# Zero fills on another engine, V's class-order transfers spread out, three products placed later: one encoder layer on one core

## The chip, the core and the metric

The kernel runs on one core of a Trainium2 chip. The core has a matrix engine (TensorE, PE), a vector engine (VectorE, DVE), an engine for activation functions (ScalarE, ACT), a general engine (GpSimd, POOL) and one that only issues transfers (SyncE, SP). Each engine executes its own instructions in order and waits at semaphores for the others. Transfers between the chip's memory and the core's are issued from an engine's queue (SPq, POOLq, ACTq) and carried out by 16 DMA engines. The metric is the device time of one execution, in microseconds (us).

## The reference

One layer of an encoder on x of shape 512 x 1024, float32. The parts that the change is near:

```
h = rms_norm(x, attn_norm_g)
xr, gate, q, k, v = split(h @ w_in)                  # 512 wide each
y_rnn  = (rg_lru(conv(xr), forward) + rg_lru(conv(xr), backward)) * gelu(gate)
y_attn = dilated_attention(q, k, v, rel_bias)        # 8 heads of 64
x = x + concat(rms_norm(y_rnn), rms_norm(y_attn)) @ w_out
x = x + square(relu(rms_norm(x) @ w_up)) @ w_down    # 4096 wide
return rms_norm(x) * final_norm_g
```

In `dilated_attention` a query looks at keys at three sets of distances: up to 64 in steps of 1, up to 256 in steps of 4, up to 1024 in steps of 16. The three softmaxes are put together by their denominators, which equals one softmax in which a key that lies in several sets counts several times.

## The kernel before

**Products.** A float32 operand is split into a high and a low part (`whi`, `wlo`: `conv_hi` on ScalarE, `conv_lo` on VectorE), and one product of a 128-row block is three matmuls (`mm3`, lines 312 to 314): high x high, high x low, low x high. Weights come in blocks of 128 x 1024 (512 KB).

**Stages.** First the projections of xr, V, gate, and Q and K of the first pair of heads, with the recurrent group's elementwise work beside them. Then attention, in pairs of heads p = 0 to 3. Then the attention half of the output projection, then the two halves of the feed-forward, whose products (`pu`, `pd`) run from about 230 us to the end.

**Attention.** Keys near a query (distance up to 64) and keys farther away (a multiple of 4) are scored apart: `att_s` computes the near scores (`pn`, line 779) for query blocks u, u+1 and, at u = 0, the far scores (`pf`, line 786). `att_f` adds the bias to the far scores of block u and writes them with their minimum into a tile `e` (line 799); `att_e` does so for the near scores (line 818), and ScalarE takes the exponential of the whole row in place (line 821). At the edges, blocks 0 and 3, 64 columns of `e` hold no score; they are filled with zero (line 803), since the transpositions that follow (`att_t`, line 833, results copied by ScalarE into `ett`, line 835) move whole 128 x 128 blocks. `att_av` multiplies with V: near blocks from `vs`, far ones from `vc`, V's rows in class order (position modulo 4), into which five transfers from `vs` sort them (`v_far`, line 723). Result `yp`, its square summed over pairs into `ysq`, its scaled copy `at`.

**Steps.** The loop goes over i = 0 to 4 and u = 0 to 3. Step (i, u) scores pair i (at u = 0 and 2) and transposes for pair i - 1; `att_av(i - 1)` stands at u = 3. In between, `fill` takes products off a queue of 80: 48 products of Q and K of pairs 1 to 3, then, after a call of `load_x`, 32 of the recurrent half of the output projection (`pwo<-whi,yh`). The table FILL says how many are taken at each of four places of a step, (1, 1, 1, 1) where it has no entry. Behind the loop come `att_av(3)`, more products, the column sums of `ysq` (`pcs`, line 411), from which the reciprocal roots `rcol` follow on VectorE, GpSimd and VectorE, and then the attention half (`pwo<-whi,oh`) in seven groups of four products, OSEQ: 11, s2, s3, s4, 21, s1, 22.

**Weight sums.** The groups s1 to s4 use sums of weight blocks. `load_x` loads a base block for each into `ws` from SP (line 1003) and adds others by accumulating transfers from GpSimd's queue (line 1005): s2 two, s3 one, s4 three, s1 one, in the order s2, s2, s3, s4, s4, s4, s1.

**What sets the order.** On TensorE, ScalarE, VectorE and GpSimd instructions run in the order in which the program is written. The queue of SP is put in order by the framework's scheduler from the data's dependences. GpSimd's queue holds, in program order, the zero fills, the accumulating transfers and the small power operation of the reciprocal roots (line 399).

## Time and profile before

| | |
|---|---|
| three runs | 553.13, 555.14, 554.56 us; median 554.56 us |
| profiled execution | 554.31 us, of it 552.5 us from the first to the last instruction (the span) |
| busy in the span | TensorE 530.6, VectorE 423.9, ScalarE 352.9, GpSimd 65.7 us |
| TensorE's waits over 1 us | 8.7 us for GpSimd, 2.2 and 1.3 us for VectorE, 1.1 us at the start |
| mean granted clock of TensorE | 0.981 |

Times in the profile are microseconds from the span's start. A row of the timeline gives start, duration, engine, line, operation, out<-in with partitions x elements, and a count; in brackets stands how long the engine sat idle before it and what ended that. Buffer numbers are left out of names. PEclk is the share of full speed that TensorE's clock was granted. Rows of matmuls that follow each other overlap: their starts say how fast they go.

### The profile page before, as it was taken

What the parts mean: (1) busy time and instruction counts of PE and PEld (TensorE: products, weight loads), DVE (VectorE), ACT (ScalarE), POOL (GpSimd) and SP (SyncE); (2) the same over time, 40 slices, a digit from 0 to 9 for tenths busy, and PEclk for the clock granted to TensorE, in tenths of its full rate; (3) what the DMA queues carried; (4) which work ended last, traced back from release to release, by engine and by line L of the source; (5) the groups of instructions that cost most, each with busy time, mean ns of one, the idle gap of its engine ahead of it and who ended that gap; (6) DMA issues with size and microseconds to landing.
All of it is one profiled execution on the core that took longest, in us unless ns stands there. A gap on an engine that the chain in (4) does not pass through costs nothing.

```text
span 552.5 us, 9169 instructions
## 1 busy us (share of the span) xinstructions
PE 530.6 (96%) x3507; PEld 452.7 (82%) x3507; DVE 423.9 (77%) x679; ACT 352.9 (64%) x557; POOL 65.7 (12%) x107
## 2 busy tenths in 40 slices
PE   9999999899999399999999999999999999999995
PEld 7856888687886367889999988888999999888884
DVE  6896886676764178789878988879857887986885
ACT  7668957657855253758657855557576776755664
POOL 3320000000010221000130031101011030131000
PEclk9999999999999689999999999999999999999998
DMA  7754169533299607774759599994897496799704
GB/s 268 233 156 130 35 174 198 141 98 101 85 332 302 127 12 157 239 286 152 191 134 218 172 222 274 277 339 162 261 268 195 149 187 177 180 306 256 191 0 152
DMA packets 34587, 104.10 MB, mean 188 GB/s; under 512 B 3981, under 2 KB 6954, under 8 KB 34544
## 3 DMA queue, kind: packets, MB, share of 16 engines
q1 hardware_dynamic: 26304, 74.66, 40.2%
q0 software_dynamic: 7920, 28.61, 27.6%
q8 instruction: 27, 0.44, 0.3%
q10 hardware_dynamic: 320, 0.25, 0.2%
q14 instruction: 16, 0.13, 0.1%
HBM read 96.15 MB, written 4.21 MB: 182 GB/s over the span
## 4 chain that ended last, share of the span: by engine, by line
PE 85%; DMA 7%; DVE 4%; ACT 1%; issue 1%; POOL 1%; SPq 0%; DVEq 0%; POOLq 0%; ACTq 0%
PE pu L314 10%; PE pu L312 10%; PE pu L313 10%; PE pd L314 9%; PE pd L312 9%; PE pd L313 9%; DMA ws<-in_w_out_dram 6%; PE pqk L312 3%; PE pqk L313 2%; PE pqk L314 2%; PE pg L502 2%; PE pv L312 1%; PE pt L833 1%; PE pv L314 1%; PE pv L313 1%; PE pp L314 1%
## 5 line engine op out<-in xcount | busy, mean ns | idle before, releaser
L268 DVE TENSOR_TENSOR wlo<-wraw,whi 128x1024 fp32r<-128x1024 f32 x73 | 89.0, 1221 | 29.9 <-ACT whi L260 29.6
L260 ACT ACTIVATE whi<-wraw 128x1024 fp32r<-128x1024 f32 x70 | 74.0, 1059 | 47.4 <-PE pd L314 20.5
L313 PE MATMUL pd<-wlo,ah 128*128 128x512 f32 (+1 forms) x195 | 75.2, 386 | 0.0
L312 PE MATMUL pd<-whi,ah 128*128 128x512 f32 (+1 forms) x195 | 75.2, 386 | 0.0
L314 PE MATMUL pd<-whi,al 128*128 128x512 f32 (+1 forms) x195 | 75.2, 386 | 0.0
L313 PE MATMUL pu<-hl,whi 128*128 128x256 f32 x224 | 63.4, 283 | 0.0
L314 PE MATMUL pu<-hh,wlo 128*128 128x256 f32 x224 | 63.4, 283 | 0.0
L312 PE MATMUL pu<-hh,whi 128*128 128x256 f32 x224 | 63.4, 283 | 0.0
L314 PE MATMUL pu<-h2h,wlo 128*128 128x256 f32 (+1 forms) x200 | 60.1, 301 | 0.2 <-DVE wlo L268 0.2
L312 PE MATMUL pu<-h2h,whi 128*128 128x256 f32 (+1 forms) x200 | 60.1, 300 | 0.0
L313 PE MATMUL pu<-h2l,whi 128*128 128x256 f32 (+1 forms) x200 | 60.0, 300 | 0.0
L260 ACT ACTIVATE whi<-tw 128x1024 fp32r<-128x1024 f32 x36 | 38.1, 1060 | 33.8 <-DMA tw<-in_w_up_dram 7.3
L268 DVE TENSOR_TENSOR wlo<-tw,whi 128x1024 fp32r<-128x1024 f32 x36 | 44.0, 1223 | 15.7 <-ACT whi L260 15.7
L312 PEld LDWEIGHTS pu<-hh,whi 128*128 128x128 f32 x224 | 43.0, 192 | 0.0
L313 PEld LDWEIGHTS pu<-hl,whi 128*128 128x128 f32 x224 | 43.0, 192 | 0.0
L314 PEld LDWEIGHTS pu<-hh,wlo 128*128 128x128 f32 x224 | 43.0, 192 | 0.0
L314 PEld LDWEIGHTS pd<-whi,al 128*128 128x128 f32 x195 | 36.6, 188 | 7.4
L313 PEld LDWEIGHTS pd<-wlo,ah 128*128 128x128 f32 x195 | 36.6, 188 | 7.4
L312 PEld LDWEIGHTS pd<-whi,ah 128*128 128x128 f32 x195 | 36.6, 188 | 7.3
L260 ACT ACTIVATE whi<-ts 128x1024 fp32r<-128x1024 f32 x24 | 25.5, 1061 | 24.7 <-PE pd L314 18.7
L314 PEld LDWEIGHTS pu<-h2h,wlo 128*128 128x128 f32 x200 | 38.3, 191 | 1.8 <-DVE wlo L268 0.6
L312 PEld LDWEIGHTS pu<-h2h,whi 128*128 128x128 f32 x200 | 38.3, 191 | 1.3
(265 smaller groups left out, 1234.6 us busy)
## 6 DMA issues: line engine op xcount, KB each, us to landing
wraw<-in_w_up_dram SPq DMA_DIRECT2D x25, 512.0 KB
ts<-in_w_dn_dram POOLq DMA_DIRECT2D x24, 512.0 KB, 13.7
wraw<-in_w_dn_dram SPq DMA_DIRECT2D x24, 512.0 KB
tw<-in_w_up_dram SPq DMA_DIRECT2D x15, 512.0 KB
tw<-in_w_up_dram POOLq DMA_DIRECT2D x15, 512.0 KB, 7.3
wraw<-in_w_in_dram SPq DMA_DIRECT2D x13, 512.0 KB
ts<-in_w_dn_dram SPq DMA_DIRECT2D x8, 512.0 KB
tw<-in_w_dn_dram SPq DMA_DIRECT2D x8, 512.0 KB
```

The lines of the kernel that those rows point to most:

```text
L260: act(hi, raws[i], AF.Copy)
L268: nc.vector.tensor_tensor(lo, r, f(splits[i][0]), op=OP.subtract)
L312: nc.tensor.matmul(o, lhsT=a[0], rhs=b[0], start=bool(first), stop=False, skip_group_check=on)
L313: nc.tensor.matmul(o, lhsT=a[0], rhs=b[1], start=False, stop=False, skip_group_check=on)
L314: nc.tensor.matmul(o, lhsT=a[1], rhs=b[0], start=False, stop=bool(last), skip_group_check=on)
L502: nc.tensor.matmul(pg[2 * d + j][halves[b ^ d]], lhsT=gwr[t][halves[b], c], rhs=xc[t][halves[b]], start=True, stop=True)
L833: nc.tensor.transpose(pt[:, i * P:(i + 1) * P], en[h][u][:, c * P:(c + 1) * P], ident)
```

## The change

Three things change, and the computation does not.

The zero fills of `att_f` (16 in all, 128 x 64) are issued on VectorE instead of GpSimd. `v_far` takes the block j as an argument and is called in steps (0, 0) to (0, 3) instead of for all j behind the gate projection. FILL takes three products instead of four in steps (3, 1), (3, 2) and (3, 3), moves the one product of step (4, 3) to its last place, and behind `att_av(3)` four are taken instead of three; what is left of the queue runs behind the column sums as before, three products instead of one.

```diff
@@ v_far
-    def v_far():
-        for j in range(4):
-            for a, b, s in (((0, P, 32 * j - 16),) if j else ((0, 64, 112), (64, P, 0))):
-                n = (b - a) // 4
-                nc.sync.dma_start(vc[s:s + n], vs[a:b, j, :])
+    def v_far(j):
+        for a, b, s in (((0, P, 32 * j - 16),) if j else ((0, 64, 112), (64, P, 0))):
+            n = (b - a) // 4
+            nc.sync.dma_start(vc[s:s + n], vs[a:b, j, :])
@@ behind the gate projection
-    v_far()
@@ att_f
-                nc.gpsimd.memset(t[:, g], 0.0)
+                nc.vector.memset(t[:, g], 0.0)
@@ the steps
-    FILL = {(4, 0): (0, 1, 0, 0), (4, 1): (0, 1, 0, 1), (4, 2): (0, 1, 0, 0), (4, 3): (0, 1, 0, 0)}
+    FILL = {(3, 1): (1, 1, 1, 0), (3, 2): (1, 1, 1, 0), (3, 3): (1, 1, 1, 0), (4, 0): (0, 1, 0, 0), (4, 1): (0, 1, 0, 1), (4, 2): (0, 1, 0, 0), (4, 3): (0, 0, 0, 1)}
     for i in range(5):
         for u in range(4):
+            if i == 0:
+                v_far(u)
@@ behind the steps
     att_av(3)
     att_y(3)
-    fill(3)
+    fill(4)
     cs = col_sums(ssy[1], "gs")
```

Lines behind `v_far` move up by one or two: the fill's line 803 becomes 801, the scores' 799 and 818 become 797 and 816.

GpSimd's queue around the weight sums `ws`, before: `e` is the score tile, `rcol` the reciprocal roots, first those of the recurrent half, then those of attention.

```order
L803 MEMSET e_1613 128x64
L803 MEMSET e_1617 128x64
L1005 DMA ws_1714<-in_w_out_dram 128x1024 x7
L803 MEMSET e_1850 128x64
L803 MEMSET e_1854 128x64
L803 MEMSET e_1909 128x64
L803 MEMSET e_1913 128x64
L399 TENSOR_TENSOR rcol_2_2206<-rv_2204,mhalf_85 128x4
L1097 DMA tw_2284<-in_w_up_dram 128x1024
```

And with the change:

```order
L399 TENSOR_TENSOR rcol_1_1579<-rv_1577,mhalf_85 128x4
L1003 DMA ws_1714<-in_w_out_dram 128x1024 x7
L399 TENSOR_TENSOR rcol_2_2199<-rv_2197,mhalf_85 128x4
L1097 DMA tw_2284<-in_w_up_dram 128x1024
L1097 DMA tw_2310<-in_w_up_dram 128x1024 x2
```

The sixteen fills are gone from it, among them four that stood behind the seven accumulating transfers.

VectorE in step (0, 1), before: from the recurrent group's last sum past the far scores of blocks 2 and 3 to the near scores of block 1, whose end frees the banks for the scores of blocks 2 and 3. `mf` and `mn` are the minima that go with the scores `e` (the numbers tell one buffer from another).

```order
L571 TENSOR_TENSOR gt_786<-gt_786,ga_470 128x512
L799 ISA e_1072,mf_1073<-pf_973,tw_641 128x128
L799 ISA mf_1073 128x1
L799 ISA e_1075,mf_1076<-pf_974,tw_644 128x128
L799 ISA mf_1076 128x1
L799 ISA e_1078,mf_1079<-pf_973,tw_641 128x128
L799 ISA mf_1079 128x1
L799 ISA e_1082,mf_1083<-pf_974,tw_644 128x128
L799 ISA mf_1083 128x1
L818 ISA e_1037,mn_1086<-pn_975,tw_641,mf_1038 128x256
L818 ISA mn_1086 128x1
```

And with the change:

```order
L571 TENSOR_TENSOR gt_786<-gt_786,ga_470 128x512
L797 ISA e_1070,mf_1071<-pf_970,tw_641 128x128
L797 ISA mf_1071 128x1
L797 ISA e_1073,mf_1074<-pf_971,tw_644 128x128
L797 ISA mf_1074 128x1
L797 ISA e_1076,mf_1077<-pf_970,tw_641 128x128
L797 ISA mf_1077 128x1
L801 MEMSET e_1076 128x64
L797 ISA e_1080,mf_1081<-pf_971,tw_644 128x128
L797 ISA mf_1081 128x1
L801 MEMSET e_1080 128x64
L816 ISA e_1034,mn_1084<-pn_972,tw_641,mf_1035 128x256
```

Two fills, those of block 3, stand here, and the two of block 0 stand in the same way in the group ahead of it; so it is in every pair.

SP's queue at the last of V's transfers (`vs<-vs`), before: `hs` are exchanges of the recurrent group, `wraw` weight blocks, `tw` the bias tables of the next pair.

```order
L243 DMA wraw_815<-in_w_in_dram 128x1024
L493 DMA hs_821<-ga_558 64x512 x2
L723 DMA vs_712<-vs_712 32x4x512
L243 DMA wraw_856<-in_w_in_dram 128x1024
L723 DMA vs_712<-vs_712 32x4x512
L243 DMA wraw_901<-in_w_in_dram 128x1024
L243 DMA wraw_938<-in_w_in_dram 128x1024
L243 DMA wraw_971<-in_w_out_dram 128x1024
L243 DMA wraw_1110<-in_w_out_dram 128x1024
```

And with the change:

```order
L243 DMA wraw_815<-in_w_in_dram 128x1024
L493 DMA hs_821<-ga_558 64x512 x2
L722 DMA vs_712<-vs_712 32x4x512
L243 DMA wraw_856<-in_w_in_dram 128x1024
L243 DMA wraw_896<-in_w_in_dram 128x1024
L243 DMA wraw_933<-in_w_in_dram 128x1024
L722 DMA vs_712<-vs_712 32x4x512
L243 DMA wraw_966<-in_w_out_dram 128x1024
L243 DMA wraw_1108<-in_w_out_dram 128x1024
```

The last of the five stands behind two more weight loads; the four ahead of it, of which the rows show one, keep their places.

## The prediction

> **What bounds the kernel now.** I read the page first, then the waits of TensorE, then its timeline at each wait, then the queue of the engine that ended the wait. From the page, the span and the busy times by engine:

> ```profile
> span 552.5 us, 9169 instructions
> PE 530.6 (96%) x3507; PEld 452.7 (82%) x3507; DVE 423.9 (77%) x679; ACT 352.9 (64%) x557; POOL 65.7 (12%) x107
> ```

> TensorE (PE) is busy for 96% of the span, so only its idle time, and the time in which it runs slowly, can be won. The longest of its waits (total us, times, longest):

> ```profile
> PE pt L833 <- POOL e L803: 8.7, 1, 8.7
> ```

> One transposition of exponentials (`att_t`) waits 8.7 us for a zero fill on GpSimd (POOL). Here it is in TensorE's timeline with the two next longest (start, duration, and in brackets the idle time before):

> ```profile
> 107.20 1.98 PE L779 MATMUL pn<-kraw,qraw 64*32 64x256 f32 x32 [2.21 <-DVE mn L818]
> ...
> 179.41 0.44 PE L833 MATMUL pt<-ident,e 128*128 128x128 f32 x2 [0.47 <-ACT ett L835]
> 188.51 1.54 PE L833 MATMUL pt<-ident,e 128*128 128x128 f32 x6 [8.66 <-POOL e L803]
> ...
> 202.71 1.23 PE L411 MATMUL pcs<-ones,ysq 128*128 128x1 f32 x8 [1.33 <-DVE ysq L588]
> ```

> ```profile
> 176.12:179.54 3.42, 2.35 (x16) 1.00 1.03 358
> 179.54:182.95 3.41, 0.30 (x2) 1.00 0.50 114
> ...
> 186.36:189.78 3.42, 1.27 (x7) 0.50 0.48 77
> 189.78:193.19 3.41, 3.41 (x12) 0.50 1.05 197
> ...
> 200.02:203.43 3.41, 2.08 (x13) 1.00 0.00 0
> 203.43:206.85 3.42, 3.42 (x10) 0.50 0.00 0
> ```

> The stretch from 200.02, with 1.33 us of idle, is followed by one at half speed; the stretch from 176.12, with 1.07 us, is not. A half-speed stretch that is busy throughout loses 1.7 us.

> **Part 1: the fills leave POOL.** This is what the 8.66 us stand behind, POOL's own timeline:

> ```profile
> 153.31 0.99 POOL L1005 DMA_DIRECT2D ws<-in_w_out_dram  x1 [10.23 <-DMA ws<-in_w_out_dram]
> ...
> 180.64 0.87 POOL L1005 DMA_DIRECT2D ws<-in_w_out_dram  x1 [13.62 <-DMA ws<-in_w_out_dram]
> 186.52 1.77 POOL L1005 DMA_DIRECT2D ws<-in_w_out_dram  x2 [5.00 <-DMA ws<-in_w_out_dram]
> 187.61 1.10 POOL L803 MEMSET e<- 128x64 f32 x4
> ```

> Seven weight sums are issued from POOL, and a sum waits for the landing of the one on which it builds. The last pair's four fills stand behind all seven and run at 187.61. On VectorE (DVE) each fill stands right behind the scores of its own tile, so nothing is left of this wait: **-8.7 us**. With it go the half-speed stretches behind it: 1.27 + 3.41 = 4.68 us busy at half speed are 2.34 us at full: **-2.3 us**. The 0.47 us ahead of 179.41, a wait for ScalarE, stays.

> What the fills cost on VectorE is not in the trace. The nearest rows, with minimum, median and maximum duration in ns:

> ```profile
> L143 DVE MEMSET ones<- x1: 165/165/165, 0.8 to 0.8; 128x128 f32 x1
> L145 DVE MEMSET epsb<- x1: 59/59/59, 1.0 to 1.0; 128x1 f32 x1
> L803 POOL MEMSET e<- x16: 141/152/849, 43.6 to 187.9; 128x64 f32 x16
> ```

> Between 59 and 165 ns a fill of 64 columns comes to 59 + 106 x 63/127 = 112 ns, an estimate. Four stand ahead of the second near-score group (`att_e`, u = 1) of every pair, and the scores of step 2 wait for that group. Where TensorE already waits, they lengthen the wait: the first pair, at 107.20, by 4 x 0.11 = **+0.4 us**. The bounds: 0.2 us if half of each fill hides under its neighbour, and 3.4 us at the 849 ns of POOL's slowest row. I take 0.4, since both VectorE rows lie far below POOL's slowest. The other pairs have cover. The rows below are, for pairs 1 to 3, the last score group on VectorE and the scores on TensorE that wait for it (0.99 us there, 1.98 us at 107.20, where the clock is half):

> ```profile
> 123.30 0.48 DVE L818 CUSTOM_DVE_ANT_0 e<-pn,tw,mf 128x256 f32<-128x256 f32 x1
> 125.46 0.99 PE L779 MATMUL pn<-kraw,qraw 64*32 64x256 f32 x32
> ...
> 142.92 0.48 DVE L818 CUSTOM_DVE_ANT_0 e<-pn,tw,mf 128x256 f32<-128x256 f32 x1
> 146.29 0.99 PE L779 MATMUL pn<-kraw,qraw 64*32 64x256 f32 x32
> ...
> 163.34 0.48 DVE L818 CUSTOM_DVE_ANT_0 e<-pn,tw,mf 128x256 f32<-128x256 f32 x1
> 166.16 0.99 PE L779 MATMUL pn<-kraw,qraw 64*32 64x256 f32 x32
> ```

> That leaves 1.7, 2.9 and 2.3 us; the last shrinks to 1.6, because part 3 takes one product away ahead of it. All exceed 0.4, so these twelve fills cost nothing.

> **Part 2: V's transfers.** The order of SP's queue shows that four of the five stay where they were; one goes behind two weight loads.

> ```profile
> 89.91 0.58 SPq L243 DMA_DIRECT2D wraw<-in_w_in_dram  x1
> 90.54 0.59 SPq L723 DMA_DIRECT2D vs<-vs  x1
> 91.23 4.74 SPq L243 DMA_DIRECT2D wraw<-in_w_in_dram  x2
> ...
> 98.72 1.06 ACT L260 ACTIVATE whi<-wraw 128x1024 fp32r<-128x1024 f32 x1 [3.85 <-DMA wraw<-in_w_in_dram]
> 99.81 1.22 DVE L268 TENSOR_TENSOR wlo<-wraw,whi 128x1024 fp32r<-128x1024 f32 x1 [3.19 <-ACT whi L260]
> 132.88 2.82 PE L914 MATMUL pav<-ett,vs 128*64 128x128 f32 x32
> ```

> The moved transfer, issued at 90.54, will be issued at about 96 (91.23 + 4.74); its reader starts at 132.88, 37 us later, so nothing is lost. Something could be won: the wait at 107.20 ends a chain on VectorE that follows the subtraction at 99.81, which waits for a load. But that is the load of 89.91, already ahead of the moved transfer. I take **0**. The bounds: no loss, and a gain of at most 1.6 us if the load should land so much earlier that the far scores start when theirs are done (99.3 instead of 100.9), which would leave 2.2 + 0.4 - 1.6 = 1.0 us of idle and so save the half-speed stretch too, 3.3 us in all.

> **Part 3: three products later.** TensorE's work is the same. Three products leave the last pair's steps 1 to 3; one of them now stands ahead of the column sums (`fill(4)` for `fill(3)`), two behind. A product is three matmuls 0.23 us apart, 0.69 us in all. Ahead of the sums runs this chain:

> ```profile
> 200.15 1.11 DVE L930 TENSOR_TENSOR yp<-pav,zrow 128x512 f32<-128x512 f32 x1
> 201.96 0.69 DVE L588 TENSOR_TENSOR ysq<-ysq 128x512 f32<-128x512 f32 x1 [0.70 <-ACT ysq L582]
> ...
> 200.53 0.39 PE L312 MATMUL pwo<-whi,yh 128*128 128x512 f32 x1
> 200.76 0.39 PE L313 MATMUL pwo<-wlo,yh 128*128 128x512 f32 x1
> ```

> The fourth product covers 0.69 of the 1.33 us; VectorE's order also has one weight subtraction (1.2 us) now behind `yp` instead of ahead of it. What is left lies between 0 and 0.64 us; I take 0.3: **-1.0 us**. That is below 1.07 us of idle, so the half-speed stretch from 203.43 goes as well: **-1.7 us**. Behind the sums three products instead of one stand over the reciprocal roots, where TensorE shows no wait even now. The moved products also carry the weight splits of groups 11, s2 and s3, and the split of 11 frees the buffer for this load:

> ```profile
> 172.34 0.33 SPq L243 DMA_DIRECT2D wraw<-in_w_up_dram  x1
> ```

> That split now stands behind `yp` on VectorE, so the load goes out some 5 us later, about 177; the feed-forward, which reads it, starts near 217 then, 40 us on.

> **What is late next.** With TensorE 13 us earlier the weight sums have less time. ScalarE reads the s4 sum at the first row below; the sum under it in the same tile took 5.35 us (from the chain of waits):

> ```profile
> 205.47 1.06 ACT L260 ACTIVATE whi<-ws 128x1024 fp32r<-128x1024 f32 x1
> ...
> 180.64 5.35 DMA ws<-in_w_out_dram
> ```

> The s4 sum lands near 186.52 + 5.35 = 191.9, and its reader comes at 205.47 - 13.3 = 192.2: in time, but barely. Its products come eleven products (7.6 us) after that read, and the split takes 2.3 of them (1.06 + 1.22, rows of part 2), so some 5 us of lateness would be absorbed.

> **The sum.** -8.7 - 2.3 + 0.4 + 0 - 1.0 - 1.7 = -13.3 us. The profiled execution took 554.31 us (1.8 outside its span), so 541.0; the median shown, 554.56, lies 0.25 higher: **541.2 us**. The stages behind shift as a whole; this row of TensorE's busy time (columns as above) shows them:

> ```profile
> 240.00:540.00 300.00, 300.00 (x1878) 1.00 0.77 206
> ```

> **The rivals.** *The half-speed stretch behind the column sums stays.* For it: 1.07 and 1.33 us of idle are close together, where the stretches begin relative to the work is open, and the sums themselves hardly occupy the array. Against it: only 0.3 us of idle remains. 541.2 + 1.7 = 542.9 us. [...]

> *V's move relieves the first pair:* 541.2 - 3.3 = 537.9 us. Against it: the load that matters was issued before the moved transfer.

> *The weight sums become the wait:* if they land 7 to 10 us later than reckoned, 2 to 5 us come back: 543 to 546 us. For it: a margin of 0.3 us at s4 before ScalarE, which holds other work in order, waits. Against it: nothing of the change delays them.

> *The weight stream gives the gain back:* if the loads of the later stages cannot follow, TensorE waits there: 554 us, no change. Against it: from 240 to 540 us TensorE never waits at a DMA share of 0.77, and loads are issued as buffers come free, so they shift with it.

> *Slower:* if a fill holds VectorE for x us, each pair loses 4x less its cover of 0, 1.7, 2.9 and 1.6 us, and stalls above 1.3 us add a half-speed stretch. At POOL's 0.85 that is 3.4 + 1.7 + 0.5 + 1.8 + 2 x 1.7 = 10.8 us, 541.2 - 0.4 + 10.8 = 551.6 us, still faster. From 1.1 us a fill on (16 x 1.1 - 6.2 + 3 x 1.7 = 16.5) it ends above 557.3 us, slower. Nothing in the VectorE rows is near that.

> **How the numbers follow.** The forecast has a chance of 0.61, the half-speed rival 0.18, V's relief 0.07, late sums 0.08, the stream 0.04, slow fills 0.02. The first two and half of the next two hold 0.86: I give 538.5 to 545.5 us, which covers the open costs (3.3 down, 1.7 and some late sums up). A measurement of this kernel tells 0.5% (2.8 us) from no change; faster by more than that 0.95, within it 0.03, slower 0.02.

> **What would show it.** No wait of a transposition for the fills, and TensorE busy between 175 and 190 us; a wait of 2.4 to 2.9 us at the first pair's second scores (about 107 us), followed by half speed; VectorE fills of about 0.11 us; under 0.7 us of idle ahead of the column sums and full clock behind them; whole stages behind unchanged in length. The prediction is wrong if TensorE waits for ScalarE's reads of `ws`, if another pair's scores wait for VectorE, or if the later stages get longer.

## The result, and the profile after

The changed kernel takes **537.9 us** (median of four executions, 537.65 to 539.04), the kernel before 553.85 us in the same comparison (552.34 to 555.14): a ratio of 0.972, 95% interval 0.969 to 0.975. The forecast was 541.2 us, with a range from 538.5: the direction and the large terms came out, the size fell short by 3.3 us, and the time lies 0.6 us below the range. The profiled execution took 539.04 us, the longest of the four, so 1.1 of the 3.3 us is the choice of execution, and 0.2 us is the step from the profiled execution before to the median that the forecast started from; 2.0 us (541.0 less 539.04) is to be found in the trace.

The page of the changed kernel, span and busy times by engine:

```profile
span 537.2 us, 9162 instructions
PE 524.9 (98%) x3507; PEld 448.3 (83%) x3507; DVE 423.3 (79%) x695; ACT 352.2 (66%) x557; POOL 64.0 (12%) x91
```

TensorE's waits after the change (total us, times, longest):

```profile
PE pn L777 <- DVE mn L816: 1.3, 1, 1.3
...
PE pwo L312 <- DVE x L1120: 1.0, 2, 0.6
...
PE pt L831 <- DVE rz L842: 0.7, 1, 0.7
PE pt L831 <- ACT ett L833: 0.4, 1, 0.4
...
PE pcs L411 <- DVE ysq L588: 0.2, 1, 0.2
```

The wait for the fills on GpSimd is gone, and the one ahead of the column sums is down from 1.3 to 0.2 us. The surprise is the first line: the first pair's second scores wait 1.3 us, where I had forecast 2.4 to 2.9. TensorE's timeline at the same places, and then the stretches of the clock (length, busy times with counts for TensorE, its weight loads, VectorE, ScalarE and GpSimd, then granted clock, DMA share, GB/s):

```profile
106.92 1.39 PE L777 MATMUL pn<-kraw,qraw 64*32 64x256 f32 x32 [1.34 <-DVE mn L816]
...
175.52 1.15 PE L831 MATMUL pt<-ident,e 128*128 128x128 f32 x8 [0.41 <-ACT ett L833]
...
187.28 1.05 PE L411 MATMUL pcs<-ones,ysq 128*128 128x1 f32 x8 [0.16 <-DVE ysq L588]
193.84 0.50 PE L312 MATMUL pwo<-whi,oh 128*128 128x512 f32 x1 [0.60 <-DVE x L1120]
```

```profile
103.34:106.75 3.41, 2.24 (x10) 1.50 (x9) 3.38 (x17) 1.58 (x2) 0.00 (x0) 1.00 0.02 6
106.75:110.17 3.42, 3.25 (x40) 2.32 (x41) 2.70 (x10) 3.36 (x9) 0.00 (x0) 1.00 0.27 65
...
178.43:181.85 3.42, 3.42 (x27) 2.77 (x27) 1.31 (x4) 3.42 (x9) 0.61 (x1) 1.00 0.64 115
...
188.67:192.09 3.42, 3.42 (x16) 2.79 (x16) 2.91 (x8) 1.22 (x2) 1.96 (x3) 1.00 0.91 175
...
235.00:530.00 295.00, 295.00 (x1849) 268.17 (x1849) 242.42 (x304) 194.25 (x280) 37.71 (x43) 1.00 0.76 204
```

No half-speed stretch is left ahead of the last few microseconds: the clock is 1.00 behind the first pair (106.75), where the fills had stalled (178.43), and behind the column sums (188.67). The 1.34 us at the first pair are as long as the wait of 1.33 us that half speed followed before, but they fall into two stretches: 1.17 us of them into the first row (3.41 less 2.24), the rest into the second. The later stages are full, as before.

To see where the 15.3 us of span went, I laid TensorE's instructions of the two traces beside each other in order and read how far each start had moved. The third column is the change at that step alone; the three products that change places (0.69 us each) are left out of it:

| place | start before -> after | what the step gave | forecast |
|---|---|---|---|
| first pair, second scores | 107.20 -> 106.92 | -0.3 | +0.4 |
| stretch behind them, now full clock | | -1.6 | 0 |
| transpositions that waited for the fills | 188.51 -> 175.79 | -8.9 | -8.7 |
| stretches behind them | | -2.2 | -2.3 |
| idle ahead of the column sums | 202.71 -> 187.28 | -1.2 | -1.0 |
| stretch behind them | | -1.5 | -1.7 |
| waits for `x` in the output products | 208.74 -> 193.84 | +0.4 | 0 |

Five lines agree within 0.4 us, and the first two, at the first pair, hold 2.3 us that the forecast did not have. Of these, 0.3 us are the fills, for which I had counted 0.4 (part 1 below). What is left is whether V's move, for which I had taken 0, is the cause of the other 2.0.

### The profile page after: what moved, and what is told of

The parts are those of the page before. It is cut to its first block, busy times and chain, and to the rows that moved or that the text cites. A ratio compares the mean times of both kernels' runs of the same rounds, so it can differ in the third digit from the quotient of the medians.

```text
span 537.2 us, 9162 instructions
## 1 busy us (share of the span) xinstructions
PE 524.9 (98%) x3507; PEld 448.3 (83%) x3507; DVE 423.3 (79%) x695; ACT 352.2 (66%) x557; POOL 64.0 (12%) x91
## 4 chain that ended last, share of the span: by engine, by line
PE 75%; DMA 10%; ACT 5%; DVE 5%; issue 2%; POOL 1%; SPq 0%; DVEq 0%; ACTq 0%; POOLq 0%
PE pu L314 10%; PE pu L313 10%; PE pu L312 10%; PE pd L312 9%; PE pd L314 9%; PE pd L313 9%; DMA ws<-in_w_out_dram 6%; DMA wraw<-in_w_in_dram 3%; PE pqk L312 2%; PE pqk L313 1%; PE pqk L314 1%; PE pg L502 1%; PE pxr L312 1%; PE pxr L314 1%; PE pxr L313 1%
## 5 line engine op out<-in xcount | busy, mean ns | idle before, releaser
L268 DVE TENSOR_TENSOR wlo<-wraw,whi 128x1024 fp32r<-128x1024 f32 x73 | 88.9, 1221 | 28.3 <-ACT whi L260 28.1
L260 ACT ACTIVATE whi<-wraw 128x1024 fp32r<-128x1024 f32 x70 | 74.0, 1059 | 44.6 <-PE pd L314 20.5
L313 PE MATMUL pd<-wlo,ah 128*128 128x512 f32 (+1 forms) x195 | 75.2, 386 | 0.0
L312 PE MATMUL pd<-whi,ah 128*128 128x512 f32 (+1 forms) x195 | 75.2, 386 | 0.0
L313 PE MATMUL pu<-hl,whi 128*128 128x256 f32 x224 | 63.4, 283 | 0.0
L312 PE MATMUL pu<-hh,whi 128*128 128x256 f32 x224 | 63.4, 283 | 0.0
L260 ACT ACTIVATE whi<-tw 128x1024 fp32r<-128x1024 f32 x36 | 38.1, 1060 | 37.0 <-DMA tw<-in_w_up_dram 10.1
L312 PE MATMUL pu<-h2h,whi 128*128 128x256 f32 (+1 forms) x200 | 60.1, 300 | 0.0
L313 PE MATMUL pu<-h2l,whi 128*128 128x256 f32 (+1 forms) x200 | 60.0, 300 | 0.0
L268 DVE TENSOR_TENSOR wlo<-tw,whi 128x1024 fp32r<-128x1024 f32 x36 | 44.0, 1222 | 17.5 <-ACT whi L260 17.5
L312 PEld LDWEIGHTS pu<-hh,whi 128*128 128x128 f32 x224 | 43.0, 192 | 0.0
L313 PEld LDWEIGHTS pu<-hl,whi 128*128 128x128 f32 x224 | 43.0, 192 | 0.0
L313 PEld LDWEIGHTS pd<-wlo,ah 128*128 128x128 f32 x195 | 36.6, 188 | 7.4
L312 PEld LDWEIGHTS pd<-whi,ah 128*128 128x128 f32 x195 | 36.6, 188 | 7.2
L260 ACT ACTIVATE whi<-ts 128x1024 fp32r<-128x1024 f32 x24 | 25.5, 1061 | 24.3 <-PE pd L314 18.1
L312 PEld LDWEIGHTS pu<-h2h,whi 128*128 128x128 f32 x200 | 38.3, 191 | 1.3
```

Of the source, the lines that this page charges most:

```text
L260: act(hi, raws[i], AF.Copy)
L268: nc.vector.tensor_tensor(lo, r, f(splits[i][0]), op=OP.subtract)
L312: nc.tensor.matmul(o, lhsT=a[0], rhs=b[0], start=bool(first), stop=False, skip_group_check=on)
L313: nc.tensor.matmul(o, lhsT=a[0], rhs=b[1], start=False, stop=False, skip_group_check=on)
```

## Experiments

**One part at a time, and two.** Theory A: V's move gave the 2 us. Rival B: it gave nothing, and the first pair did better by chance in the one execution profiled. Against the kernel before, the four kernels have these edits:

```diff
 # fills only:                 -  nc.gpsimd.memset(t[:, g], 0.0)
                               +  nc.vector.memset(t[:, g], 0.0)
 # fills and V:                and v_far() split into v_far(u), called in step u of the first pair
 # fills and products:         and the changed FILL table, fill(4) for fill(3)
 # V only:                     only v_far(u)
```

> The kernel before with its fills moved to VectorE, nothing else. Theory A (the 2 us that the forecast lacked come from V's move, at the first pair's second scores): this kernel has no part of them; the wait there stays at 2.2 us or a little more and is followed by a half-speed stretch, the wait for the fills (8.7 us) and the half speed behind it (2.2 us) are gone, the 1.3 us ahead of the column sums and its half-speed stretch stay: about 543.0 us. Rival B (V's move does nothing; the first pair gained by where the clock's stretches or the loads happened to fall in one execution): the first pair is already better here, 541.1 us. Either way a fill that takes its full 0.11 us of VectorE would lengthen the first pair's score chain by 0.4 us; hidden beside the scores, by less than 0.1.

> Fills on VectorE and V's transfers spread, the three products left where they were. Theory A: 1.8 us under the kernel with the fills alone (about 541.1 us), with a first-pair wait below 1.5 us and full clock behind it; the column sums as before (1.3 us idle, then half speed). Rival B: the same time as the fills alone, within 0.5 us.

> The changed kernel without V's move: fills on VectorE, the three products later, V's transfers as before. Theory A: 1.8 us over the changed kernel, about 539.7 us, with 2.2 us of idle at the first pair's second scores and half speed behind it. Rival B: 537.9 us, the changed kernel's time. In both, under 0.7 us of idle ahead of the column sums and full clock behind them, and some 3 us less than with the fills alone.

> The kernel before with V's transfers spread, nothing else. Theory A: the first pair gains 1.8 us, but the transpositions still wait for the fills on GpSimd, whose time is set by the weight sums ahead of them and not by TensorE; the wait grows by the gain (8.7 to 10.5 us), and the time stays at 553.9 us. If the sums move up with TensorE it is 552.0 us. Rival B: 553.9 us with a first-pair wait of 2.2 us and half speed behind it.

Measured, all on one chip, medians of 6 to 17 executions: before 553.1, fills only 541.2 (ratio 0.979, 0.974 to 0.984), fills and V 540.0, fills and products 538.9, V only 551.1 us (0.996, 0.993 to 0.999). So the fills alone are worth 11.9 us, the products some 2.3, V's move between 1.2 and 2.0. A third way to price V's move gives less: the changed kernel, run next on the same chip, took 538.6 us, 0.3 under fills and products alone. The executions of one kernel spread over 2.5 to 8 us, so none of these differences of V's move is settled here, and the profiles did not look as theory A had it. With the fills alone:

```profile
PE pcs L411 <- DVE ysq L588: 1.3, 1, 1.3
...
PE pn L779 <- DVE mn L818: 0.9, 1, 0.9
```

A first-pair wait of 0.9 us without V's move, not 2.2, and no half speed anywhere ahead of the end, not even behind the 1.3 us at the column sums. Theory A in its simple form fell with this. This profile is a lucky draw, though: it is the fastest of its six executions (538.46 us), and by mean clock (0.991 to 0.994 against 0.997) each of the other five had one or two half-speed stretches more. In the kernel with V's move alone the fills' wait did not grow by what the first pair gained:

```profile
184.44 1.54 PE L831 MATMUL pt<-ident,e 128*128 128x128 f32 x6 [8.15 <-POOL e L801]
```

TensorE came earlier, the weight sums on GpSimd too, and the wait stayed at 8 us; the expectation's second branch.

**Where the load lands.** The load that the first pair's far scores wait for was issued at 89.91 us before and at 89.99 after, ahead of the moved transfer both times. From the DMA completions in the traces I read when it landed, and when the transfer of V issued just ahead of it had landed. That gave theory C: both the landing and the place of the clock's stretches vary from execution to execution, and V's move shortens the time between the two landings. It was put to second profiles of both kernels.

> The kernel before once more, for a second profile of it. Theory C (the load ahead of the first pair's far scores lands at a time that varies by about 1 us between executions, and a half-speed stretch follows only where at least some 1.3 us of idle fall into one stretch of 3.41 us): the first pair's wait lies between 0.9 us, as with the fills alone, and 2.2 us, as in the profile before; half speed behind it only if it is over 1.3 us; the mean clock is 0.981 with that stretch and 0.984 to 0.988 without it. In any case the load lands 1.8 us or more behind the transfer of V ahead of it. Theory A (without V's move the wait is 2.2 us): 2.2 us and half speed again.

> The changed kernel once more, beside the others. Theory C: 537.5 to 539 us, a mean clock of 0.996 to 0.999 (no half-speed stretch but the one at the end), the first pair's wait between 0.6 and 1.4 us, the load landing 1.0 to 1.2 us behind the transfer of V ahead of it. Against the kernel with fills and products alone (538.9) that is under 1 us: V's move is worth about 0.4 us plus a share of the 1.7 us of a half-speed stretch. Theory A: 1.8 us under that kernel.

Measured: 552.3 us for the kernel before (first-pair wait 2.1 us, half speed behind it) and 538.6 us for the changed one (0.9 us, full clock). Later runs gave more profiles (their expectations follow below), and together they separate cleanly:

| profile | V's transfer landed | load landed | between | first-pair wait | clock behind it |
|---|---|---|---|---|---|
| before (three profiles) | 96.3, 96.6, 96.2 | 98.6, 98.8, 98.7 | 2.3, 2.2, 2.5 | 2.2, 2.1, 2.4 | half, half, half |
| fills only | 95.4 | 97.2 | 1.8 | 0.9 | full |
| changed without V's move (three) | 95.9, 97.6, 96.8 | 97.7, 100.2, 99.1 | 1.8, 2.6, 2.3 | 1.1, 3.6, 1.9 | full, half, half |
| changed (three) | 97.2, 96.1, 96.3 | 98.3, 97.1, 97.3 | 1.0, 1.0, 1.0 | 1.3, 0.9, 1.1 | full, full, full |
| fills and V | 95.7 | 96.9 | 1.2 | 0.7 | full |
| V only | 95.2 | 96.4 | 1.2 | 0.6 | full |

Without V's move 1.8 to 2.6 us pass between the landings, with it 1.0 to 1.3 (two further kernels below that keep V's moved transfers on SP's queue, with the fivefold fills and with a later end of the recurrence, lie at 1.0 and 1.3). In the two profiles compared above, the load itself landed only 0.3 us earlier, since the transfer ahead of it landed 0.9 us later; over seven profiles with V's move and seven without, it landed 1.3 us earlier (97.3 against 98.6 in the mean). The stretch from 95 to 100 us, of the kernel before and then of the changed kernel, points to the reason:

```profile
95.00:100.00 5.00, 5.00 (x110) 3.90 (x109) 1.81 (x3) 1.26 (x2) 0.00 (x0) 1.00 1.03 245
```

```profile
95.00:100.00 5.00, 4.75 (x109) 3.78 (x108) 2.74 (x3) 2.71 (x4) 0.00 (x0) 1.00 0.94 307
```

The 16 DMA engines are busy almost throughout there (shares 1.03 and 0.94). Before, the fifth transfer of V (issued 0.63 us behind the load) is in flight with the load; the engines are as busy and move fewer bytes (245 against 307 GB/s). After, the transfer goes out at 97.26, and of the three loads in the first row the second follows the one that matters 1.17 us behind it (91.16):

```profile
89.99 7.22 SPq L243 DMA_DIRECT2D wraw<-in_w_in_dram  x3
97.26 0.60 SPq L722 DMA_DIRECT2D vs<-vs  x1
...
98.38 1.06 ACT L260 ACTIVATE whi<-wraw 128x1024 fp32r<-128x1024 f32 x1 [2.27 <-DMA wraw<-in_w_in_dram]
```

So it is not any transfer behind the load that holds it up: a weight load follows it in both kernels (at 91.23 before), and only V's transfer between the two is gone (2.3 us between the landings before, 1.0 after). The rates bear it out in all fourteen profiles: from 95 to 100 us the engines moved 201 to 281 GB/s without V's move and 307 to 337 with it, at shares of 0.94 to 1.05.

**The queue or the engines?** Two kernels move V's five transfers to another queue.

```diff
-            nc.sync.dma_start(vc[s:s + n], vs[a:b, j, :])
+            nc.gpsimd.dma_start(vc[s:s + n], vs[a:b, j, :])    # V off SP
+            nc.scalar.dma_start(vc[s:s + n], vs[a:b, j, :])    # V late, behind a weight split on ScalarE
```

> The changed kernel with all five transfers of V issued from GpSimd's queue, which has nothing to do at that time. If the place in SP's queue is what V's transfers cost the loads, the load ahead of the far scores lands up to 4 us earlier, before 95 us, the far scores start when their matmuls end (99.3 us), and the first pair's wait is about 0.6 us in every execution; time 0.2 to 0.7 us under the changed kernel. If the transfers only share the DMA engines, the landing hardly moves (96.5 us or later), and so does nothing else.

> The changed kernel with V's five transfers issued from ScalarE's queue, where they stand behind the weight split of about 98 us, and so behind the loads. Theory D (from 90 to 100 us the 16 DMA engines are full, and every transfer issued ahead of the load or close behind it holds its landing up, whichever queue it stands in): with no transfer of V in that time the load ahead of the far scores lands by 95 us instead of 97 to 98, the far scores start when their matmuls end (99.3 us), and the first pair's wait is 0.6 us, no more, in any execution. Time 0 to 0.7 us under the changed kernel (538.6). Rival E (the order in SP's queue alone counts): the same landing as when GpSimd's queue issued them, 99 us, and the same time of 540 us.

From GpSimd's queue all five transfers go out by 87.2 us, ahead of the load (88.3). It landed at 99.0, later than in the kernel before, though SP's queue held nothing of V; the wait was 2.5 us with half speed behind it, and the time 540.0 us. From ScalarE's queue two go out at 94 to 95 us, the others later; the load landed at 93.0, and the wait was 0.7 us. The time was 538.1 us, the changed kernel's within its spread. The DMA share and GB/s, first from GpSimd's queue, then from ScalarE's:

```profile
90.00:95.00 5.00, 5.00 (x24) 4.14 (x23) 2.44 (x4) 3.01 (x4) 0.00 (x0) 1.00 1.04 147
95.00:100.00 5.00, 5.00 (x111) 3.89 (x109) 0.67 (x1) 0.89 (x1) 0.00 (x0) 1.00 1.01 309
```

```profile
90.00:95.00 5.00, 5.00 (x24) 4.13 (x22) 2.43 (x4) 3.82 (x5) 0.00 (x0) 1.00 0.60 197
95.00:100.00 5.00, 5.00 (x111) 3.90 (x109) 2.03 (x3) 1.43 (x2) 0.00 (x0) 1.00 0.88 254
```

Neither branch of the first expectation holds as written: the landing neither came forward 4 us nor stayed, it went back. Theory D fits both as far as they go: with V's five transfers ahead of the load on GpSimd's queue the share from 90 to 95 us is 1.04 at 147 GB/s, and the load is late (99.0 us); with none of V's in flight beside it the share is 0.60, and the load is early (93.0 us). That a transfer close behind the load holds it up is shown on SP's queue alone; one close behind it on another queue was not run.

**The price of a fill.**

```diff
-                nc.vector.memset(t[:, g], 0.0)
+                for _ in range(5):
+                    nc.vector.memset(t[:, g], 0.0)
```

> The changed kernel with every fill done five times over on VectorE (four of the five do nothing). It prices a fill: the forecast had 0.11 us each, all of it on the path of the first pair's second scores, so 16 more there are 1.8 us more of wait (2.7 us in all, and half speed behind it: 3.5 us over the changed kernel). If a fill mostly hides beside the score operations as the traces now show (0.02 us in sequence for one), the first is nearly free but the repeats, which have nothing to hide beside, show their own pitch of about 0.06 us: 1 us more of wait, 1 to 2.7 us in time.

It took 549.2 us, 10.6 more than the changed kernel (538.6): both guesses were far too low. The rows of the changed kernel, one fill between score groups:

```profile
105.42 0.28 DVE L797 CUSTOM_DVE_ANT_0 e<-pf,tw 128x128 f32<-128x128 f32 x1
...
106.10 0.11 DVE L801 MEMSET e<- 128x64 f32 x1
106.13 0.23 DVE L797 CUSTOM_DVE_ANT_0 e<-pf,tw 128x128 f32<-128x128 f32 x1
...
106.32 0.11 DVE L801 MEMSET e<- 128x64 f32 x1
106.35 0.41 DVE L816 CUSTOM_DVE_ANT_0 e<-pn,tw,mf 128x256 f32<-128x256 f32 x1
```

and of the one with five, with TensorE's wait that they end in:

```profile
107.86 0.88 DVE L802 MEMSET e<- 128x64 f32 x5
108.66 0.23 DVE L797 CUSTOM_DVE_ANT_0 e<-pf,tw 128x128 f32<-128x128 f32 x1
...
110.21 2.15 PE L777 MATMUL pn<-kraw,qraw 64*32 64x256 f32 x32 [4.60 <-DVE mn L817]
```

A fill lasts 0.11 us, as estimated, but the next operation starts 0.03 us after the fill's start. A repeat on the same columns costs (0.80 - 0.03) / 4 = 0.19 us, where the second guess took 0.06, a figure that no row shows; sixteen of them at the first pair are 3.1 us, and the wait grew by 3.3 (4.60 against 1.34). So one fill beside a score operation costs 0.03 us or less here, and the repeats priced something else; why a repeat costs more was not tried. With the slow clock behind it, the first pair accounts for 4.6 of the 10.6 us. The other 6.0 come behind it: sixteen repeats a pair (3.1 us) are more than the cover of 1.7, 2.9 and 1.6 us reckoned for the later pairs, and TensorE now waits 0.8 us at the scores of two of them, and 0.8 and 1.3 us at transpositions. The scores' waits in all (total us, times, longest):

```profile
PE pn L777 <- DVE mn L817: 6.2, 3, 4.6
```

**The last operations of a recurrence behind the scores.** The first pair's wait ends on VectorE whatever the load does, so it can also be shortened there.

```diff
-    plan = {..., (0, 0, 3): [end(1)], (0, 1, 1): [sq_(1)], ...
+    plan = {..., (0, 1, 0): [end(1)], (0, 1, 2): [sq_(1)], ...
```

> The changed kernel with one thing more: the two elementwise operations that end the second recurrence (0.69 + 0.69 us on VectorE, issued every 1.3 us) stand behind the second score group of the first pair and not ahead of it. The wait of the first pair's second scores (0.6 to 1.3 us) is ended by VectorE, so it should go: 0.6 to 1.3 us under the changed kernel, 537 us, and no half-speed stretch there whatever the landing. Rival: TensorE then waits 0.6 us or more later on for the weight split or the scores that are 1.3 us later on VectorE, and the time stays.

It took 537.8 us, 0.8 less than the changed kernel beside it (538.6), with no wait at the first pair and none in its place. The four executions of each overlap (536.9 to 539.0 against 538.0 to 539.2), so the time alone does not show the gain; the trace shows that the wait is gone.

**V's move by time, and both cures together.** Two more profiles of single executions, and then, on one chip, the changed kernel, the same without V's move, and the changed kernel with the two last edits together.

> The kernel before, a third profile. Theory D: 1.8 us or more between the two landings; first-pair wait 0.9 to 2.2 us. If it is near 2.1 a third time, while the kernels without V's move and with the fills on VectorE again stay near 1.0, then the fills have a part in the landing after all, which the traces so far do not explain.

> The changed kernel without V's move once more, for a second profile of the load's landing. Theory D: 1.8 us or more between the landing of V's transfer and that of the load behind it (1.0 to 1.3 us with V's move), at a DMA share of 1.0 from 90 to 100 us; first-pair wait between 0.9 and 2.2 us; if it is over 1.3 us and within one stretch of the clock, half speed behind it.

> The changed kernel, to be compared with the next one on the same chip. Theory D: 537.9 to 538.6 us, a first-pair wait of 0.6 to 1.4 us and no half speed behind it, 1.0 to 1.3 us between the landing of V's transfer and that of the load behind it.

> The changed kernel without V's move. Theory D: 1.8 to 2.6 us between the two landings, a first-pair wait of 0.9 to 3.6 us, half speed behind it in more than half of the executions; in the mean of its executions 2 us (1 to 3) over the changed kernel, with a wider spread of times. If it is within 0.5 us of the changed kernel, V's move isn't what the forecast lacked, whatever single profiles show.

> The changed kernel with V's transfers issued from ScalarE's queue behind the weight split, and the end of the second recurrence behind the second score group. Theory D: the load lands by 95 us, no wait at the first pair's second scores, no half-speed stretch there; 0.6 to 1.3 us under the changed kernel, 537.0 to 537.8 us. Rival: other waits at the start (1 us for the first warm-up products, up to 1.2 us for ScalarE's first split) vary by as much, and the time is the changed kernel's.

The two single profiles are in the table above: a third wait of 2.4 us before (556.1 us), and 3.6 us without V's move (542.65 us), so long waits come with the fills on either engine. Of the three, six executions each: changed 538.3 us (537.9 to 538.8), without V's move 539.8 us (538.8 to 543.6), both edits 537.2 us (536.7 to 538.2). Every execution without V's move is longer than every one with it, the closest by 0.05 us; the means differ by 2.2 us (95% interval 0.3 to 4.1, from the spread of the two sixes). Over all executions of the two kernels in every comparison, 13 without and 14 with V's move, the means differ by 1.7 us (0.7 to 2.8), and there the times overlap. By mean clock (0.991 and 0.993 against 0.996 and more) two of the six had a half-speed stretch more, not over half of them as expected. One of the two is the profiled one, first its stretch from 95 to 100 us and then two stretches of the clock:

```profile
95.00:100.00 5.00, 5.00 (x111) 3.98 (x109) 2.17 (x2) 1.20 (x2) 0.00 (x0) 1.00 1.00 225
105.88:109.29 3.41, 1.52 (x33) 0.91 (x34) 3.35 (x17) 1.79 (x6) 0.00 (x0) 1.00 0.00 0
109.29:112.71 3.42, 3.42 (x9) 2.65 (x9) 1.64 (x5) 3.29 (x7) 0.00 (x0) 0.50 0.42 158
```

The kernel with both edits has no wait left at that place:

```profile
105.84 0.99 PE L777 MATMUL pn<-kraw,qraw 64*32 64x256 f32 x32
```

Its mean is 1.0 us under the changed kernel's (0.5 to 1.6); against the kernel before its ratio is 0.971 (0.967 to 0.975). That is 0.2%, the best of those run; how much each of the two edits gives was not separated.

## Why the prediction fell short, point by point

**Part 1, the fills (-8.7, -2.3, +0.4).** The first two terms came out (-8.9 and -2.2). The third was a sixth of what I took: the duration of 0.11 us was right to the third digit (112 ns in all 16 rows), but the chain of scores with its four fills grew by only 0.07 us (0.88 against 0.84 us in the first group of far scores, 1.50 against 1.47 from the second group to TensorE's start). The starts of the two groups and of the near scores behind the first, before and then after:

```profile
100.96 0.28 DVE L799 CUSTOM_DVE_ANT_0 e<-pf,tw 128x128 f32<-128x128 f32 x1
...
101.80 0.41 DVE L818 CUSTOM_DVE_ANT_0 e<-pn,tw,mf 128x192 f32<-128x192 f32 x1
...
105.73 0.28 DVE L799 CUSTOM_DVE_ANT_0 e<-pf,tw 128x128 f32<-128x128 f32 x1
```

```profile
100.61 0.28 DVE L797 CUSTOM_DVE_ANT_0 e<-pf,tw 128x128 f32<-128x128 f32 x1
...
101.49 0.42 DVE L816 CUSTOM_DVE_ANT_0 e<-pn,tw,mf 128x192 f32<-128x192 f32 x1
```

Where these operations overlap, the duration was not the price: 0.45 us for four fills against 0.07. The lower bound named, 0.2, was still too high.

**Part 2, V's transfers (0): the step that failed.** I wrote that the load that matters "is the load of 89.91, already ahead of the moved transfer", and so took 0. Order in the queue was the wrong test. The transfer behind the load held it up at a DMA share of 1.03, and moving it let the load land some 0.6 to 1.6 us sooner behind its predecessor. With that the first pair's wait is 0.6 to 1.3 us and not 0.9 to 3.6, and full clock follows it in all five such profiles of the table. By time that is 2.2 us side by side (0.3 to 4.1). That V's transfer did it is shown by taking its move out; that it did so by sharing the engines is read from the rates (245 and 307 GB/s in the two profiles) and not shown apart. The bounds given, 0 to 3.3 us, held the value; I chose the wrong end. The range did not follow these bounds either: I wrote that it covered 3.3 us down, but 541.2 - 3.3 = 537.9 us lies below its lower end of 538.5, and the measured time fell into that gap. The row that spoke against me was to be had: the DMA share of 1.03 from 95 to 100 us.

**Part 3, the products (-1.0, -1.7).** Right in both (-1.2 and -1.5), though the second is not there in every execution: with the fills alone the same 1.3 us ahead of the column sums was followed by full clock. The output products now wait 0.4 us more for `x` on VectorE (0.60 us at 193.84), which I had not seen and did not follow up.

**What is late next.** Right, with more room than reckoned: the weight sums moved up with TensorE (the first of the last pair goes out at 184.3 us, not 186.5), the s4 sum landed at 189.7 and was read at 191.2. The split that frees the `wraw` buffer went behind `yp` as said, and its load went out at 175.4.

**The rivals.** *V's move relieves the first pair* is what happened, and I had given it a chance of 0.07. That its time (537.9) is the measured one to the tenth is luck: it put 3.3 us on V's move, the runs show about 2, and the rest is what the fills did not cost and the spread between single executions. The half-speed stretch behind the column sums did not stay; that the sums hardly occupy the array was my estimate from their shape (128x1), and no run shows what it does to the clock. Late weight sums, a stream that gives the gain back, and slow fills are not in the traces of the changed kernel.

**The sum.** The terms were taken against one execution with five half-speed stretches. The executions of the kernel before run from 549 to 558 us with mean clocks of 0.990 to 0.978, about one stretch of 1.7 us apart each 0.003; those of the changed kernel, fourteen in all, lie between 537.65 and 539.17 us with 0.996 to 0.999. Without waits over 1.34 us in its profiles the changed kernel has lost not only time but spread, and I had kept one such wait in the forecast.

## What to carry to other kernels

Ask of a transfer not only which loads stand behind it in its queue, but which are in flight beside it where the DMA share is near 1: here a load that was issued 0.63 us ahead of another transfer landed 2.3 us behind its predecessor, and 1.0 us without that transfer. Price an operation by the distance between starts in a chain, not by its duration (here 0.03 us against 0.11). A wait can cost more than it shows (here 1.33 us of idle brought 1.5 us more at half speed), and whether it does can differ between executions (1.34 us with the fills alone brought none), so one profile of such a place is one draw.

## What the runs showed of the hardware that I had not expected

**In two profiles the clock's fall fits idle time read 0.6 us ahead of its stretches.** In the kernel with V's move alone, a stretch with 1.62 us of idle is not followed by half speed, though 1.33 us was before:

```profile
173.56:176.97 3.41, 1.79 (x9) 1.08 (x9) 3.00 (x8) 2.21 (x4) 0.32 (x1) 1.00 0.86 332
176.97:180.39 3.42, 0.00 (x0) 0.00 (x0) 0.00 (x0) 0.00 (x0) 0.55 (x1) 1.00 0.68 116
172.96:176.37 3.41, 2.26 (x13) 1.31 (x12) 3.06 (x7) 2.21 (x4) 0.00 (x0) 1.00 0.98 362
```

Read 0.6 us earlier (the third row) it has 1.15 us of idle. The third profile of the kernel before has two stretches of this kind, each with the one behind it, and then both read 0.6 us earlier:

```profile
178.58:182.00 3.42, 1.79 (x9) 1.08 (x9) 2.85 (x8) 2.21 (x4) 0.09 (x1) 1.00 0.82 319
182.00:185.41 3.41, 0.00 (x0) 0.00 (x0) 0.00 (x0) 0.00 (x0) 0.79 (x1) 1.00 0.60 96
202.48:205.89 3.41, 2.06 (x13) 1.55 (x12) 2.23 (x5) 1.24 (x2) 0.07 (x1) 1.00 0.00 0
205.89:209.30 3.41, 3.41 (x9) 2.64 (x9) 1.84 (x6) 1.88 (x3) 2.86 (x3) 0.50 0.26 19
177.98:181.40 3.42, 2.12 (x12) 1.17 (x10) 3.07 (x8) 2.21 (x4) 0.00 (x0) 1.00 0.95 358
201.88:205.29 3.41, 2.06 (x14) 1.51 (x12) 2.51 (x4) 1.24 (x2) 0.00 (x0) 1.00 0.00 0
```

In its own stretch 1.63 us of idle brought no half speed and 1.35 us did; read earlier the first has 1.30 us, the second still 1.35. The profiles before and after agree with this shift, but do not need it: up to 525 us half speed stood behind the three full-clock stretches with 1.33, 2.21 and 3.11 us of idle (1.33, 2.21 and 2.97 read earlier) and behind none of the others, which have at most 1.17 us. The shift is chosen to fit the stretches named here; what the clock counts is not shown. Single waits that half speed stood behind are those of 1.33 and 2.21 us before, of 2.05 and 2.36 us in its two further profiles, of 1.91 us in the last profile without V's move and of 2.49 us with V's transfers on GpSimd's queue.

**Landings vary between executions of the same kernel.** The load ahead of the far scores landed at 97.7, 100.2 and 99.1 us in three executions of the changed kernel without V's move; what sets this was not tried.
